# The first input tiles and the first weight chunk in smaller parts, the second linear's chunks split inside the first, rope tables and masks ahead of the third

## The chip, the cores and the metric

The kernel runs on one core of one Trainium2 chip, as one program. The metric is the device time of one execution in microseconds; shown are the median of three runs and one profiled execution. The engines are named as in the profile: PE (TensorE matmul; PEld its weight load), DVE (VectorE), ACT (ScalarE), POOL (GpSimd) and SP (SyncE, which here only issues DMAs).

## The reference

Two layers of a decoder trunk for 256 tokens of width 1024, all in float32. Each layer:

```
h = rmsnorm(x, mix_norm);  z = h @ w_in          # split among three mixers
A: compressed / selected / windowed attention, B: windowed attention with sinks,
C: low-rank attention with a rotary key          # rotary embeddings from positions
g = sigmoid(h @ w_branch_gate)                   # g_a, g_b, g_c
x = x + (g_a*(o_a @ w_a) + g_b*(o_b @ w_b) + g_c*(o_c @ w_c)) @ w_out
x = x + (silu(h2 @ w_gate) * (h2 @ w_up)) @ w_down        # h2 = rmsnorm(x)
x = x + sigmoid(rmsnorm(x) @ w_ple_gate) * (p[i] @ w_ple_proj)
```

and a last rmsnorm. The rotary tables are cos and sin of positions times fixed frequencies.

## The kernel before, in words

**Linears.** Every weight is cut on the host into chunks of 128 partitions by up to 1024 columns, usually two slices k of the contraction by 512 output columns, laid out in the order of use. A float32 product is made of three matmuls on float32r operands: the weight is split into a high part `wh` (a rounded copy by ACT, L276) and a low part `wl` (the difference, by DVE, L281), the activations into `hT` high and low in the same way. For each token tile t (0 or 1, 128 tokens) and each k, `lin` (L331) issues the matmuls high by `wh`, high by `wl`, low by `wh`, in this order (L347 to L349), into a bank `lin` of PSUM. The order over t and k goes in blocks; the first linear alone takes blocks of two k, [2, 2, 2, 2] (L334). The order of the first linears of a layer is `gc0` (a gate), `g1` (low-rank inputs), `g2` (keys, rotated), `g3`, ... (L35). `gc0` has chunks 0 to 3, `g1` 4 to 7, `g2` 8 to 11.

**Chunks.** `load_to` (L253) issues the DMA of a chunk on SP into one of 4 raw buffers; `upper` (L265) issues the `wh` cast and returns a `rest` that issues the `wl` difference and, with it, the load of the chunk four later. There are 6 buffers of high and low parts. A planner (`Plan`, L76) holds modelled times of each engine while the program is written out; `feed` (L285) splits the next chunks as soon as the modelled engines are free, and `W.push` (L138) puts off a piece of work until its modelled inputs are there. `W.until` (L159) lets the model run on until a flag is set. All instructions of an engine run in the order in which they were written out.

**Start.** SP issues in this order: x tile 0 left half, chunk 0, x tile 1 left half, chunk 1, both right halves, chunks 2 and 3 (L387 to L396). ACT issues the constants `con` (identity and frequencies, 176 columns) and the layer parameters `lp`; POOL issues positions, masks (`mload`) and `con2`. PE runs filler matmuls (`warm`, L1268) on a tile of ones, 7, 4 and 4 (L1340). Around them `parts` (L1276) transposes four 128x128 blocks of one input quarter (t, g), multiplies them by the norm's gain on DVE (`xg`, gain from `lp`), casts them on ACT and makes the low part on DVE. `start_1` and `start_2` (L1297, L1305) are hung into the first linear by `script`: they are written out just ahead of the matmuls of (t, k) = (1, 0) and (0, 2) and hold the other input quarters, the splits of chunks 2 to 4, the squares of the rows of x (for the norm's factor `r`, made by POOL in `rsqrt`, L478), the last step of the rotary tables and the masks.

**Rotary tables.** `setup_rope` and `finish_rope` (L421, L446) write a chain of 16 POOL instructions that reduces the angles; `rope_rest` (L454) ends it: a maximum on DVE, one POOL instruction, two sines on ACT (which need another table of functions), and eight copies on POOL to `tabs`. The evacuation of `g2` (`ev_g2`, L662) waits for `tabs`, scales them (`rt`) and rotates; copies `kd` and four or two transposes into a bank `sc` follow.

**Evacuation of the first linear.** `gate` (L639) takes the tanh of the bank on ACT with the scale `rh` = r/2, which POOL makes after `rsqrt`. It is written out right behind the last matmul of its tile, so ACT's later casts stand behind it.

Of the kernel before, what the change touches and what calls it, by code (L numbers as in the profile page):

```python
# [8 lines left out]
F32 = mybir.dt.float32  # L9
F32R = mybir.dt.float32r  # L10
# [7 lines left out]
P = 128  # L18
# [35 lines left out]
RAWB = 4  # L54
# [11 lines left out]
C_ID, C_FREQ, C_FIRST = 0, 128, 176  # L66
# [151 lines left out]
def build(tc, wst, xin, pin, posn, cst, lpar, fnorm, out):  # L218
# [34 lines left out]
    def load_to(n):  # L253
        while st["dma"] < min(n, len(CHUNKS)):
            i = st["dma"]
            off, kk, c = CHUNKS[i]
            r = sb([P, 1024], name="raw", bufs=RAWB, p=wp)
            nc.sync.dma_start(out=r[:, :kk * c],
                              in_=wst[off:off + P * kk * c].rearrange("(p n) -> p n", p=P))
            W.op("D", kk * c * P * 4 / 350e3, [r.tensor.name], [])  # L260
            W.end[r.tensor.name] = ("D", W.t["D"] + 2.0)
            raws[i] = r
            st["dma"] += 1
# [38 lines left out]
    def split_to(n):  # L302
        st["goal"] = max(st["goal"], n)
        feed()
# [26 lines left out]
    def lin(l, name, nk, lhs, evac, blocks=None, wait=0.0, halves=False):  # L331
# [5 lines left out]
        for b in blocks:  # L337
            for t in range(2):
                if t and halves:
                    break  # L340
                for k in range(k0, k0 + b):
# [6 lines left out]
                    T.matmul(out=o, lhsT=xh, rhs=wl, start=False, stop=False)  # L348
                    T.matmul(out=o, lhsT=xl, rhs=wh, start=False, stop=(k == nk - 1))  # L349
# [28 lines left out]
    con = sb([P, C_FIRST], name="con")  # L378
    con2 = sb([P, C_N], name="con2")
# [20 lines left out]
    ident = con[:, C_ID:C_ID + P]  # L400
# [200 lines left out]
    def layer(l, nm, nxt):  # L601
# [120 lines left out]
        step["g2"] = lambda: lin(l, "g2", 8, nm.lhs, ev_g2)  # L722
# [540 lines left out]
    nm = Norm(lps[0][:, L_MIX:L_MIX + 8])  # L1263
# [32 lines left out]

    def start_1():  # L1297
        nm.square(0, 0)
        nm.square(1, 0)
        w2 = split(2)  # L1300
        lo = parts(0, 1)
        w2()
        lo()

    def start_2():  # L1305
        w3 = split(3)
        lo = parts(1, 1)
        w3()
        lo()
        w4 = split(4)  # L1310
        nm.square(0, 1)
        w4()
        nm.square(1, 1)
        rope_t["last"]()
        W.push([], setup_masks, 20.0)
        split_to(HLB)

    warm(WARM[0])
    lo = parts(0, 0)
    w0 = split(0)  # L1320
    lo()
    warm(WARM[1])
    lo = parts(1, 0)
    w0()
    warm(WARM[2])
    w1 = split(1)
    lo()
    w1()
    script[1, 0] = [start_1]
    script[0, 2] = [start_2]  # L1330
    for l in range(DEPTH):
        nm = layer(l, nm, None)
# [7 lines left out]
WARM = (7, 4, 4)  # L1340
# [4 lines left out]
def host_layout(inputs):  # L1345
# [50 lines left out]
    con[:, C_ID:C_ID + P] = np.eye(P)  # L1396
# [37 lines left out]
```

## Time and profile before

| | us |
|---|---|
| median of three runs | 962.79 (962.58 to 962.92) |
| profiled execution, its own time | 962.83 |
| span of the profiled execution | 961.0 |

Times in the rows below count from the start of the span. A row of a timeline has the start, the time taken, the engine, the line of the kernel, the operation, output and inputs by the program's names (buffer numbers left out), shapes and a count. Nearly all instructions show line L214, since a helper records each of them, so they are told apart by tiles. In brackets stands the idle time of the engine before the instruction and what ended it. A matmul's end is modelled and overlaps the next one's start.

### The profile page before, as it was taken

Reading aid. Unit: us, or ns where it says so; the run is one execution under the profiler, and the core shown is the slowest. Engines: PE = TensorE matmul, PEld = TensorE weight load, DVE = VectorE, ACT = ScalarE, POOL = GpSimd, SP = SyncE. Lnnn points to the kernel's source line nnn. Section 1 sums busy time; section 2 is a strip of 40 time slices with the busy share of each in tenths; the row PEclk is TensorE's granted clock in tenths of the full one; section 3 lists DMA queues with packets and bytes.
Section 4 is the critical chain, followed back from the end, with each engine's and each line's share of the span. In section 5 each row is a group of like instructions: output and inputs, shape, how many; then the busy total and the mean of one; then the engine's idle time right before and its main releaser. Section 6 shows DMA issues by size and latency. Waiting matters only on the chain.

```text
span 961.0 us, 13658 instructions
## 1 busy us (share of the span) xinstructions
PE 946.2 (98%) x4867; PEld 781.2 (81%) x4867; DVE 670.1 (70%) x1226; ACT 560.7 (58%) x1015; POOL 53.3 (6%) x104
## 2 busy tenths in 40 slices
PE   8999999999999999999999999999999999999996
PEld 5788888777888888888888898877778888888886
DVE  6696788668776666654767868876886766665554
ACT  6668857666554445443665686766655544444444
POOL 7200000000010000000121000000000000000010
PEclk9999999999999999999999999999999999999999
DMA  8557534525455555657454665254245655555551
GB/s 286 159 162 228 191 102 144 168 88 196 159 187 199 179 176 175 202 170 210 161 173 155 201 200 173 89 175 153 89 154 181 204 190 193 193 179 188 185 175 44
DMA packets 46595, 164.28 MB, mean 171 GB/s; under 512 B 5504, under 2 KB 5760, under 8 KB 46528
## 3 DMA queue, kind: packets, MB, share of 16 engines
q1 hardware_dynamic: 45648, 161.80, 51.5%
q0 software_dynamic: 448, 1.30, 0.4%
q8 instruction: 38, 0.62, 0.3%
q10 hardware_dynamic: 432, 0.32, 0.1%
q14 instruction: 29, 0.24, 0.1%
HBM read 162.35 MB, written 1.05 MB: 170 GB/s over the span
## 4 chain that ended last, share of the span: by engine, by line
PE 95%; POOL 2%; ACT 1%; DVE 1%; issue 1%; ACTq 0%; POOLq 0%
PE lin L214 80%; PE tr L214 7%; PE sc L214 4%; PE pv L214 3%; PE hidps L214 2%; POOL kq L214 1%; POOL ang L214 0%; DVE wl L214 0%; POOL kp L214 0%; DVE um L214 0%; ACT xf L214 0%; DVE khA L214 0%; POOL nsk L214 0%; DVE U L214 0%; ACT pT L214 0%
## 5 line engine op out<-in xcount | busy, mean ns | idle before, releaser
L214 PE MATMUL lin<-wh,hT 128*128 128x512 f32 (+2 forms) x1600 | 512.0, 389 | 0.2 <-ACT wh L214 0.2
L214 DVE TENSOR_TENSOR wl<-raw,wh 128x1024 fp32r<-128x1024 f32 (+2 forms) x308 | 369.1, 1209 | 88.3 <-ACT wh L214 81.8
L214 ACT CAST wh<-raw 128x1024 fp32r<-128x1024 f32 (+2 forms) x308 | 315.7, 1035 | 133.9 <-PE lin L214 124.7
L214 PEld LDWEIGHTS lin<-wh,hT 128*128 128x128 f32 x1600 | 297.1, 188 | 56.7 <-issue 1.5
L214 PE MATMUL lin<-wl,hT 128*128 128x512 f32 (+2 forms) x800 | 305.3, 382 | 2.1 <-DVE wl L214 2.1
L214 PEld LDWEIGHTS lin<-wl,hT 128*128 128x128 f32 x800 | 150.8, 189 | 27.5 <-DVE wl L214 2.7
L214 PE MATMUL lin<-wh,hd 128*128 128x512 f32 x352 | 110.9, 392 | 0.0
L214 PEld LDWEIGHTS lin<-wh,hd 128*128 128x128 f32 x352 | 66.1, 188 | 13.6
L214 PE MATMUL lin<-wl,hd 128*128 128x512 f32 x176 | 68.5, 389 | 0.0
L214 PE MATMUL lin<-wh,oT 128*128 128x512 f32 x192 | 66.3, 400 | 0.0
L214 ACT ACTIVATE th<-lin,rh 128x256 f32<-128x256 f32 (+1 forms) x52 | 26.2, 503 | 65.8 <-PE lin L214 65.8
L214 ACT ACTIVATE p<-p,negm 128x256 f32<-128x256 f32 (+1 forms) x128 | 56.8, 447 | 0.0
L214 DVE SCALAR_TENSOR_TENSOR th<-th,lin 128x256 f32<-128x256 f32 x44 | 18.4, 418 | 49.5 <-ACT th L214 49.5
L214 DVE CUSTOM_DVE_ANT_0 p<-sc,masks 128x128 f32<-128x128 f32 (+1 forms) x96 | 29.5, 353 | 23.0 <-PE sc L214 23.0
L214 ACT COPY pT<-tr 128x512 f32<-128x512 f32 x48 | 28.1, 585 | 27.5 <-PE tr L214 27.1
L214 PEld LDWEIGHTS lin<-wh,oT 128*128 128x128 f32 x192 | 36.1, 188 | 6.9
L214 PE MATMUL lin<-wh,mT 128*128 128x512 f32 x128 | 41.6, 396 | 0.0
L214 POOL TENSOR_SCALAR n0v<-ssq 128x1 f32<-128x1 f32 x7 | 2.1, 304 | 699.9 <-ACT junk L214 699.8
L214 PEld LDWEIGHTS lin<-wl,hd 128*128 128x128 f32 x176 | 33.1, 188 | 6.7
L214 PE MATMUL lin<-wl,oT 128*128 128x512 f32 x96 | 37.5, 391 | 0.0
L214 DVE TENSOR_TENSOR xg<-tr,lp 128x512 f32<-128x512 f32 x28 | 19.3, 690 | 25.2 <-PE tr L214 19.6
L214 ACT CAST hd<-tr 128x256 fp32r<-128x256 f32 x44 | 16.2, 369 | 33.6 <-PE tr L214 33.6
(206 smaller groups left out, 1018.7 us busy)
## 6 DMA issues: line engine op xcount, KB each, us to landing
raw<-wst SPq DMA_DIRECT2D x296, 512.0 KB, 4.2
raw<-wst SPq DMA_DIRECT2D x8, 312.0 KB, 3.1
raw<-wst SPq DMA_DIRECT2D x4, 384.0 KB, 3.1
x<-xin SPq DMA_DIRECT2D x4, 256.0 KB, 6.1
w<-lpar POOLq DMA_DIRECT2D x2, 256.0 KB, 3.7
pr<-pin POOLq DMA_DIRECT2D x2, 256.0 KB, 4.1
fn<-fnorm SPq DMA_DIRECT2D x1, 512.0 KB, 4.1
out<-xf SPq DMA_DIRECT2D x2, 256.0 KB, 2.0
```

The lines of the kernel that those rows point to most:

```text
L214: return fn(*a, **k)
```

## The change

The identity for transposes is no longer loaded with the constants but made on POOL by a memset and a select, ahead of POOL's DMAs; the constants shrink from 176 to 56 columns and now carry the first norm's gain. The load of chunk 0 is cut in two halves, and so are its `wh` and `wl`. The left quarters of x are scaled and split from PSUM in pieces of 128x128: high part on ACT with the gain as scale, low part on DVE. Tile 1's transposes move behind the first three matmuls. In the first linear alone the low activations by `wh` come before the high ones by `wl`. The hooks move to (0, 1), (0, 2), (1, 2), (0, 6) and (1, 6), and the splits of chunks 5, 6 and 7 stand in them. The end of the rotary chain and the masks move to the start of `g2`. Filler matmuls: 7 and 3.

```
@@ -63,7 +63,7 @@
 LEAD, GAP = 128, 256
 
 
-C_ID, C_FREQ, C_FIRST = 0, 128, 176
+C_GAIN, C_FREQ, C_FIRST = 0, 8, 56
 C_CB, C_CM, C_MV, C_S, C_J, C_N = 0, 32, 64, 192, 224, 228
 C_BAND, C_CAUS, C_ALL = 0, 128, 256
 
@@ -255,8 +255,9 @@
             i = st["dma"]
             off, kk, c = CHUNKS[i]
             r = sb([P, 1024], name="raw", bufs=RAWB, p=wp)
-            nc.sync.dma_start(out=r[:, :kk * c],
-                              in_=wst[off:off + P * kk * c].rearrange("(p n) -> p n", p=P))
+            src = wst[off:off + P * kk * c].rearrange("(p n) -> p n", p=P)
+            for o in (slice(0, c), slice(c, kk * c)) if i == 0 else (slice(0, kk * c),):
+                nc.sync.dma_start(out=r[:, o], in_=src[:, o])
             W.op("D", kk * c * P * 4 / 350e3, [r.tensor.name], [])
             W.end[r.tensor.name] = ("D", W.t["D"] + 2.0)
             raws[i] = r
@@ -345,8 +346,9 @@
                     xh, xl = lhs(t, k)
                     o = banks[t][:, :c]
                     T.matmul(out=o, lhsT=xh, rhs=wh, start=(k == 0), stop=False)
-                    T.matmul(out=o, lhsT=xh, rhs=wl, start=False, stop=False)
-                    T.matmul(out=o, lhsT=xl, rhs=wh, start=False, stop=(k == nk - 1))
+                    pair = ((xh, wl), (xl, wh))
+                    for x_, w_ in pair[::-1] if c0 == 0 else pair:
+                        T.matmul(out=o, lhsT=x_, rhs=w_, start=False, stop=(k == nk - 1 and (x_ is xl) == (c0 != 0)))
                     if k == nk - 1:
                         evac(t, banks[t])
                     if t == 1 and (k % kp == kp - 1 or k == nk - 1):
@@ -376,6 +378,10 @@
 
     x = [[sb([P, 512], name=f"x{t}{g}") for g in range(2)] for t in range(2)]
     con = sb([P, C_FIRST], name="con")
+    ident = sb([P, P], name="ident")
+    G.memset(ident, 0.0)
+    G.affine_select(out=ident, in_=ident, compare_op=ALU.not_equal, fill=1.0, base=0, pattern=[[-1, P]],
+                    channel_multiplier=1)
     con2 = sb([P, C_N], name="con2")
     pos = sb([P, 2], I32, name="pos")
     lps = {}
@@ -397,7 +403,6 @@
     mload = sb([P, 2, P], name="mload", tag="kall", bufs=3)
     load(nc.gpsimd, mload, cst[:, C_FIRST + C_N:].rearrange("p (a b) -> p a b", a=2))
     load(nc.gpsimd, con2, cst[:, C_FIRST:C_FIRST + C_N])
-    ident = con[:, C_ID:C_ID + P]
     identr = sb([P, P], F32R, name="identr")
     masks = sb([P, 4, P], name="masks")
     tabs = sb([P, 2, 192], name="tabs")
@@ -719,7 +724,13 @@
                 flags.add(f"U{i}")
             W.push([Uh[i]], rest, 0.0, [uf])
 
-        step["g2"] = lambda: lin(l, "g2", 8, nm.lhs, ev_g2)
+        def step_g2():
+            if l == 0:
+                rope_t["last"]()
+                setup_masks()
+            lin(l, "g2", 8, nm.lhs, ev_g2)
+
+        step["g2"] = step_g2
 
         def ev_g3(t, b):
             rope(b[:, 0:32].rearrange("p (a b) -> p a b", a=1), 1, 16, rt[t][:, 128:192],
@@ -1260,7 +1271,7 @@
         return n4
 
 
-    nm = Norm(lps[0][:, L_MIX:L_MIX + 8])
+    nm = Norm(con[:, C_GAIN:C_GAIN + 8])
     wrm = sb([P, 512], BF16, name="wrm", tag="junk")
     V.memset(wrm, 1.0)
     wps = ps("pv")
@@ -1294,40 +1305,85 @@
             upper(i)
         return late.get(i, lambda: None)
 
+    def tr_x(t):
+        b = ps("tr")
+        for k in range(4):
+            transpose(b[:, k * P:(k + 1) * P], x[t][0][:, k * P:(k + 1) * P])
+        return b, nm.place(t, 0)
+
+    def hi_x(bo, ks):
+        for k in ks:
+            S.activation(out=bo[1][:, 0, k], in_=bo[0][:, k * P:(k + 1) * P], func=AF.Copy, scale=nm.gain[:, k:k + 1])
+
+    def lo_x(bo, ks):
+        for k in ks:
+            V.scalar_tensor_tensor(out=bo[1][:, 1, k], in0=bo[0][:, k * P:(k + 1) * P], scalar=nm.gain[:, k:k + 1],
+                                   in1=bo[1][:, 0, k].bitcast(F32), op0=ALU.mult, op1=ALU.subtract)
+
+
+
+    S.copy(out=small(1, "first", 1), in_=wrm[:, 0:1])
+    warm(WARM[0])
+    x0 = tr_x(0)
+    r0 = raws.pop(0)
+    st["split"] = 1
+    hls[0] = h0, l0 = tuple(sb([P, 1024], F32R, name="w" + p, tag=f"w{p}0") for p in "hl")
+    near, far = (0, 1), (2, 3)
+
+    def half_hi(h):
+        S.copy(out=h0[:, h], in_=r0[:, h])
+
+    def half_lo(h):
+        V.tensor_tensor(out=l0[:, h], in0=r0[:, h], in1=h0[:, h].bitcast(F32), op=ALU.subtract)
+
+    first, second = slice(0, 512), slice(512, 1024)
+    hi_x(x0, near)
+    half_hi(first)
+    lo_x(x0, near)
+    half_lo(first)
+    half_hi(second)
+    half_lo(second)
+    hi_x(x0, far)
+    nm.ok.add((0, 0))
+    warm(WARM[1])
+
     def start_1():
-        nm.square(0, 0)
-        nm.square(1, 0)
+        x1 = tr_x(1)
+        hi_x(x1, near)
+        lo_x(x1, near)
+        lo_x(x0, far)
+        load_to(RAWB + 1)
+        w1 = split(1)
+        w1()
+        hi_x(x1, far)
+        lo_x(x1, far)
+        nm.ok.add((1, 0))
+
+    def start_2():
         w2 = split(2)
         lo = parts(0, 1)
+        lo()
         w2()
-        lo()
-
-    def start_2():
+
+    def start_3():
         w3 = split(3)
         lo = parts(1, 1)
+        lo()
         w3()
-        lo()
+        nm.square(0, 0)
+        nm.square(0, 1)
         w4 = split(4)
-        nm.square(0, 1)
+        nm.square(1, 0)
+        nm.square(1, 1)
         w4()
-        nm.square(1, 1)
-        rope_t["last"]()
-        W.push([], setup_masks, 20.0)
-        split_to(HLB)
-
-    warm(WARM[0])
-    lo = parts(0, 0)
-    w0 = split(0)
-    lo()
-    warm(WARM[1])
-    lo = parts(1, 0)
-    w0()
-    warm(WARM[2])
-    w1 = split(1)
-    lo()
-    w1()
-    script[1, 0] = [start_1]
+        split(5)()
+
+
+    script[0, 1] = [start_1]
     script[0, 2] = [start_2]
+    script[1, 2] = [start_3]
+    script[0, 6] = [lambda: split(6)()]
+    script[1, 6] = [lambda: split(7)()]
     for l in range(DEPTH):
         nm = layer(l, nm, None)
     W.until(lambda: len(sent) == 2)
@@ -1337,7 +1393,7 @@
 SPACE = 4.2
 SLACK = 0.9
 TWO = "ga"
-WARM = (7, 4, 4)
+WARM = (7, 3)
 NEAR = 2
 WAIT = 1.5
 
@@ -1393,7 +1449,7 @@
     lp = np.ascontiguousarray(np.stack(lp))
     i = np.arange(P)
     con, con2, con3 = (np.zeros((P, n), np.float32) for n in (C_FIRST, C_N, C_ALL))
-    con[:, C_ID:C_ID + P] = np.eye(P)
+    con[:, C_GAIN:C_GAIN + 8] = lp[0][:, L_MIX:L_MIX + 8]
     con3[:, C_CAUS:C_CAUS + P] = np.where(i[None, :] <= i[:, None], 0, NEG)
     con3[:, C_BAND:C_BAND + P] = np.where(i[None, :] > i[:, None], 0, NEG)
     fr = [10000.0 ** (-np.arange(0, d, 2) / d) for d in (64, 32)]
```

## Rows read from the trace of the kernel before

**Rows 1.** The page, part 1: busy time, share of the span and instructions of each engine.

```profile
PE 946.2 (98%) x4867; PEld 781.2 (81%) x4867; DVE 670.1 (70%) x1226; ACT 560.7 (58%) x1015; POOL 53.3 (6%) x104
```

**Rows 2.** The busy time of each engine in the stretch from 10 to 20 us, its instructions, the granted clock, the DMA share and GB/s.

```profile
10.00:20.00 10.00, 9.82 (x47) 8.13 (x48) 9.08 (x12) 8.49 (x16) 9.14 (x13) 1.00 0.81 295
```

**Rows 3.** What TensorE waited for between 0 and 30 us: total us, times, longest us.

```profile
PE lin L214 <- DVE wl L214: 2.1, 2, 1.2
...
PE lin L214 <- ACT wh L214: 0.2, 1, 0.2
```

**Rows 4.** The same view from 30 us to the end, its longest entry.

```profile
PE sc L214 <- ACT kTC L214: 1.1, 2, 0.6
```

**Rows 5.** The timeline of the SP queue from 0 to 45 us (start us, us, queue, line, operation): its first input half, first weight chunk, second weight chunk.

```profile
0.72 0.38 SPq L373 DMA_DIRECT2D x<-xin  x1
1.16 0.42 SPq L258 DMA_DIRECT2D raw<-wst  x1
...
2.10 0.44 SPq L258 DMA_DIRECT2D raw<-wst  x1
```

**Rows 6.** DMA issues of three narrow stretches (0.5 to 1, 1 to 1.3 and 1.8 to 2.3 us), with KB and us from issue to landing: the first input half, the first weight chunk, the second weight chunk.

```profile
x<-xin SPq DMA_DIRECT2D x1, 256.0 KB, 3.6
...
raw<-wst SPq DMA_DIRECT2D x1, 512.0 KB, 4.7
...
raw<-wst SPq DMA_DIRECT2D x1, 512.0 KB, 7.0
```

**Rows 7.** The timeline of all engines, the start: start us, us, engine, line, operation, count, and in brackets the idle time before it and what ended it.

```profile
4.60 0.66 PE L214 MATMUL tr<-con,x 128*128 128x128 f32 x4 [0.17 <-DMA con<-cst]
...
6.13 0.69 DVE L214 TENSOR_TENSOR xg<-tr,lp 128x512 f32<-128x512 f32 x1 [4.75 <-DMA lp<-lpar]
...
8.48 0.50 PE L214 MATMUL lin<-wh,hT 128*128 128x512 f32 x1
...
10.18 0.50 PE L214 MATMUL lin<-wl,hT 128*128 128x512 f32 x1 [1.20 <-DVE wl L214]
```

**Rows 8.** Instruction groups by shape, of ScalarE: count, busy us, mean ns of one.

```profile
L214 ACT CAST wh<-raw 128x1024 fp32r<-128x1024 f32 x296 | 307.1, 1047 | 132.4 <-PE lin L214 124.0 <-DMA raw<-wst 4.3 <-DVE mg L214 2.2
...
L214 ACT CAST hT<-xg 128x512 fp32r<-128x512 f32 x24 | 14.8, 619 | 26.1 <-DVE xg L214 26.1
...
L214 ACT ACTIVATE v<-lin,n0y 128x128 f32<-128x128 f32 x2 | 0.7, 370 | 0.0
```

**Rows 9.** The same view, of VectorE.

```profile
L214 DVE TENSOR_TENSOR wl<-raw,wh 128x1024 fp32r<-128x1024 f32 x296 | 359.4, 1224 | 80.9 <-ACT wh L214 74.4 <-issue 0.3
...
L214 DVE TENSOR_TENSOR cs_s<-sc,cs_s 128x128 f32<-128x128 f32 x4 | 1.2, 291 | 0.1
```

**Rows 10.** The timeline of all engines, around the end of the first linear and in the second.

```profile
18.09 0.39 PE L214 MATMUL lin<-wl,hT 128*128 128x512 f32 x1
...
18.77 0.39 PE L214 MATMUL lin<-wl,hT 128*128 128x512 f32 x1
...
20.70 1.28 ACT L214 ACT_TABLE_LOAD   x1
...
22.42 0.28 ACT L214 ACTIVATE cs<-kq 128x96 f32<-128x96 f32 x1 [0.44 <-POOL kq L214]
...
24.69 0.69 ACT L214 ACTIVATE gateC<-lin,rh 128x512 f32<-128x512 f32 x1
...
25.23 1.38 POOL L214 COPY tabs<-cs 128x64 f32<-128x64 f32 x8
25.27 1.04 ACT L214 CAST wh<-raw 128x1024 fp32r<-128x1024 f32 x1
...
26.37 0.49 PE L214 MATMUL lin<-wh,hT 128*128 128x512 f32 x1 [0.19 <-ACT wh L214]
...
27.74 0.50 PE L214 MATMUL lin<-wl,hT 128*128 128x512 f32 x1 [0.88 <-DVE wl L214]
...
28.78 0.62 PE L214 MATMUL lin<-wh,hT 128*128 128x512 f32 x2
```

**Rows 11.** The timeline of GpSimd from 0 to 26 us.

```profile
6.43 0.18 POOL L214 CAST pf<-pos 128x2 f32<-128x2 int32 x1 [3.22 <-DMA pos<-posn]
...
12.34 0.45 POOL L214 TENSOR_SCALAR kp<-kq 128x96 f32<-128x96 f32 x1
...
13.33 1.32 POOL L214 TENSOR_SCALAR kp<-kq 128x96 f32<-128x96 f32 x1
...
21.06 1.33 POOL L214 TENSOR_SCALAR kq<-kq 128x96 f32<-128x96 f32 x1
22.48 0.32 POOL L214 TENSOR_SCALAR n0v<-ssq 128x1 f32<-128x1 f32 x1
...
23.54 0.24 POOL L214 TENSOR_SCALAR rh<-n0y 128x1 f32<-128x1 f32 x1
...
25.08 0.21 POOL L214 MEMSET masks<- 128x128 f32 x1
```

**Rows 12.** The timeline in the third linear: the rotation of its first evacuated tile, the copies after it, and the transposes of those copies on TensorE.

```profile
41.04 0.69 DVE L214 TENSOR_TENSOR ra<-lin,rt 128x512 f32<-128x512 f32 x1 [0.81 <-PE lin L214]
...
43.16 0.93 ACT L214 COPY kd<-kall 128x512 f32<-128x512 f32 x2 [4.26 <-DVE kall L214]
...
44.92 0.82 PE L214 MATMUL sc<-con,kd 128*128 128x128 f32 x6
```

## Prediction

> **What bounds the kernel now.** I read the busy shares first: TensorE (PE) is busy 946.2 us of the 961.0 us span [rows 1]. I then asked what PE waited for. After 30 us its longest single wait is 0.6 us and the largest group sums to 1.1 us [rows 4], so nothing behind 30 us is worth a change, and work saved on the other engines there is free cover. Before 30 us it loses 2.1 us to VectorE's low parts of weights (`wl`) and 0.2 us to ScalarE's high parts (`wh`) [rows 3], and before that it does no useful matmul until 8.48 us [rows 7]. So the change can move the end by what PE gains or loses in the first 30 us, one for one, and by what it disturbs later. The granted clock is 1.00 from 10 to 20 us, the full level of 2.4 GHz, after the seven filler matmuls at the start [rows 2]; I count no term for it.
>
> The same stretch shows VectorE busy 9.08 of 10 us, ScalarE 8.49 and GpSimd 9.14 [rows 2]: the start is nearly bound by all of them at once. A new order of work there mostly trades one wait for another, and that is where I expect most of an earlier start to go.
>
> **The pitch.** Two successive `wl` matmuls stand 0.68 us apart with two others between [rows 10], so one matmul of 512 columns is 0.227 us of PE. A linear of 48 is 10.9 us.
>
> **Where I measure.** The last place where the old prologue loses time is the fourth weight chunk of the second linear. The `wh` cast for it starts at 25.27 behind the tanh of the gate at 24.69, which stands behind two table loads (1.28 us each) and the sines. PE waits at 26.37 and again at 27.74 [rows 10]. The first matmul of token tile 1 of the second linear is the second of the pair at 28.78, so it starts 0.23 later, at 29.01. I work out when the changed kernel reaches that matmul.
>
> **The start, step by step.** The first input half lands at 0.72 + 3.6 = 4.32 us [rows 5, 6]. Before, the four transposes started at 4.60 because the constants with the identity came last [rows 7]; the identity is now made on GpSimd while the input is on its way. The memset of 128x128 is 0.21 us [rows 11]; the select has no row. Its lower bound is 0.2, its upper bound the slowest GpSimd row of 96 columns, 1.33 us [rows 11], taken to 128 columns: 1.8 us. I take 0.3, near the memset, since VectorE is idle then; either way it is ready before 4.32. So the transposes run at 4.47, bound by the filler matmuls, and end 0.66 later, at 5.13. The gain vector now comes with the small constants, so the wait of VectorE for `lp` until 6.13 [rows 7] goes. ScalarE then makes two pieces of 128x128 (0.37 us each, the form of `v<-lin` [rows 8], the second starting about 0.1 before the first ends): 5.17 to 5.81. The half-chunk cast of 512 columns costs what `hT` costs, 0.62 [rows 8]: 5.71 to 6.33. The half chunk is there by then, since the whole chunk landed at 1.16 + 4.7 = 5.86 [rows 5, 6]. First real matmul: 6.37 instead of 8.48, **2.1 us earlier**. The `wl` matmul, now third, waits for VectorE: 6.37 + 0.69 (a line between 0.29 at 128 and 1.22 at 1024 columns [rows 9]) = 7.06; stall 0.3 instead of the 1.2 idle before 10.18 [rows 7]. The split of the load in two costs one more issue slot on SP, 0.42 to 0.44 us [rows 5], for everything behind it; the second chunk is late by its transfer anyway (next step), so I take 0 and keep 0.4 as the bound.
>
> **The rest of the first linear.** I walked the three queues in program order with these durations. The second chunk landed at 2.10 + 7.0 = 9.1 us [rows 5, 6], which an earlier start does not speed up; `wh` 9.1 to 10.1, `wl` 10.1 to 11.4, while PE arrives at 10.8: stall 0.6. Behind it VectorE has the order low part of the input, `wl`, gain product, low part, `wl`, and twice waits about 0.8 for a ScalarE cast in between: stalls 0.6 before the third `wl`, 0.4 and 0.5 for the last input tile. Sum of stalls 2.4. Three groups of four transposes that stand in the stream cost 0.47 each, 1.4 in all. The first linear ends at 6.37 + 10.9 + 1.4 + 2.4 = 21.05. Before: counting 18 matmuls back from the first lost slot of the second linear (26.37 less 0.35 idle, so 26.02) gives 21.93. Of the 2.1 us won at the start **0.9 is left here**.
>
> **The second linear.** Its chunks 4 to 7 are now split inside the first; the sines, two table loads (1.28 each [rows 10]) and masks stand behind it and no longer precede the gate's tanh. What is late next is the tanh's scale, `rh`, from GpSimd, since the cast of chunk 7 stands behind that tanh. Before, `rh` ended at 23.78, 1.30 after its chain began at 22.48 [rows 11]. The last range-reduction step in front of it (1.33 at 21.06) moves away; the position load waits for the identity, +0.5. So `rh` = 23.78 - 1.33 + 0.5 = 22.95; tanh 22.99 to 23.68; cast to 24.63; `wl` to 25.91; PE arrives at 25.4: stall 0.6. The twelve matmuls of chunks 4 and 5, and all others of tile 0, add 24 x 0.227 = 5.45: 21.05 + 5.45 + 0.58 = 27.08, against 29.01: **1.93 us earlier**.
>
> That `rh` takes GpSimd's pace as before. The same GpSimd instruction took 0.45 us at 12.34 and 1.32 us at 13.33 [rows 11], and the slow ones fall on VectorE's `wl`. From `pf` at 6.43 to the moved step at 21.06 [rows 11] 18 instructions take 14.6 us; at 0.45 each they would take 8.1, so 6.5 is stretch. VectorE was busy 0.91 of that time [rows 2]; in my walk it waits about 5 of 15 us, so 0.67: a quarter of the stretch, 1.6 us, goes. Then `rh` is no longer last, the stall of 0.6 goes, and the end is 26.5: **2.5 us**. The Trainium skill (GPSIMD Engine Reference, 1. Specifications) says that GpSimd shares its SBUF interfaces with VectorE and contends with instructions of two SBUF inputs; by that the sum is 2.5, by an unchanged pace 1.93, and the trace agrees (0.45 against 1.32). I take 2.2 between them.
>
> **The third linear.** The chain of position tables now starts with it: a maximum on VectorE, a step on GpSimd (up to 1.33 [rows 11]), a table load 1.28, two sines of 0.28 and eight copies of 1.38 in all [rows 10], with 0.3 for the maximum: 4.8 us. It starts at 32.5 (29.01 - 2.2 + 24 matmuls and a group of transposes) and ends at 37.3 if nothing stands in front on ScalarE; the rotation that needs it starts at 41.04 - 2.2 = 38.8 [rows 12]. It is hidden, with 1.5 us to spare, and the second table load falls into ScalarE's idle time ahead of the next tanh. I cost it at 0. The masks are needed far later: 0. The dummy copy on ScalarE only occupies an idle engine: 0. Swapping the order of the second and third matmul in the first linear is what makes the late `wl` cheap, and is in the stalls above.
>
> **Sum.** The profiled execution took 962.83 us (961.0 of span and 1.83 around it); the median of the runs is 962.79, so they agree. 962.83 - 2.2 = **960.6 us**. A measurement of this kernel can tell about 0.2% from no change, 1.93 us here, so my own two ends (1.93 and 2.5) lie on and just over that line.
>
> **Rivals.**
>
> A, *the start runs nearly without stalls.* PE could reach the matmul at 6.37 + 72 x 0.227 + 1.4 = 24.1 if all 2.4 us of stalls went. For it: mask and constant loads now enter later, the small constants are 60 KB less, so the second chunk can land earlier. Against it: VectorE's order. With half the stalls gone the gain is 3.6: 959.2. Chance 0.17.
>
> B, *the table chain is late and PE waits in the third linear.* ScalarE may have in front of the sines an evacuation, two squares and two casts, 3.2 us; then the tables are 1.7 late. The copies of the rotated tile end at 44.09 and PE's transposes of them start at 44.92 [rows 12], which leaves 0.8: PE waits 0.9. Gain 1.3: 961.5. Chance 0.2. The Trainium skill (ScalarE: Activation LUTs, Rules for kernel authors) budgets about 2.7 us for each switch of tables. By that the wait would be 1.4 longer and the gain gone, about 962.8. The trace disagrees: the tanh starts at 24.69 right after a load that took 1.28.
>
> C, *GpSimd's `rh` comes a microsecond later than 22.95,* through a late position load. Then chunk 7 waits as before and the gain is 0.9: 961.9. Chance 0.08.
>
> D, *slower: the identity comes late.* Everything now starts from a select on GpSimd. From 4.47 us on, each microsecond that it is late delays every matmul by one. Break-even is 6.7 us, and from 8.6 us on the kernel is slower by over 0.2%. It would have to take 7 us from GpSimd's start at 1.2, four times the bound from the slowest row. Time: about 965. Chance 0.05.
>
> **How the numbers follow.** My own case has 0.5; with ends at 1.6 and 2.8, three quarters of it lie beyond the line: 0.38. With A: faster 0.55. Same: 0.12 + B 0.2 + C 0.08 = 0.40. Slower: D, 0.05. The range leaves out D and the far half of A: from 959.0 to 962.5, which takes in B by the trace, C, and the extra SP slot. The likeliest case alone is 960.0 to 961.2.
>
> **What would show it.** First matmul of the first linear near 6.4; three or four PE waits of 0.3 to 0.6 for `wl` or the last input tile between 10 and 18; no table load before the gate's tanh; that tanh near 22 to 23; tile 1 of the second linear from 26.5 to 27.1; no PE wait of over 0.5 from 30 to 50. I am wrong if the stalls between 7 and 21 sum to under 1 or over 3.5, or if PE waits for the key copies in the third linear.

## The result: slower by 6.5 us, and the profile after

The changed kernel takes 969.21 us (median of four runs, 967.41 to 970.18) against 962.71 before: ratio 1.0065, 95% interval 1.0048 to 1.0083. Its profiled execution took 969.15, with a span of 967.4 against 961.0. I had forecast 960.6.

**The start came as forecast.** The first real matmul runs at 6.16 [rows 7 have 8.48], GpSimd's `rh` ends at 20.59 [rows 11 have 23.78], and the second linear's tile 1 starts at 26.56, 2.44 us earlier than before. TensorE, ScalarE and GpSimd in the timeline of all engines of the changed kernel (the identity first):

```profile
0.72 0.20 POOL L214 MEMSET ident<- 128x128 f32 x1 [0.29 <-POOLq L1482]
1.00 0.29 POOL L214 TENSOR_SCALAR_AFFINE_SELECT ident<-ident 128x128 f32<-128x128 f32 x1
...
6.16 0.73 PE L214 MATMUL lin<-wh,hT 128*128 128x512 f32 x2 [0.57 <-ACT wh L214]
...
20.36 0.23 POOL L214 TENSOR_SCALAR rh<-n0y 128x1 f32<-128x1 f32 x1
...
21.75 0.67 ACT L214 ACTIVATE gateC<-lin,rh 128x512 f32<-128x512 f32 x1
...
27.50 1.04 ACT L214 CAST wh<-raw 128x1024 fp32r<-128x1024 f32 x1 [2.37 <-DMA raw<-wst]
28.45 0.68 ACT L214 ACTIVATE zc<-lin,n0y 128x512 f32<-128x512 f32 x1
...
29.18 0.66 PE L214 MATMUL tr<-ident,zc 128*128 128x128 f32 x4 [1.11 <-ACT zc L214]
```

The last three rows are the first loss: ScalarE waits 2.37 us for the transfer of chunk 9, whose cast stands in front of the evacuation `zc`, and TensorE waits for `zc`. The load of a chunk is issued behind the `wl` of the chunk four earlier; here that `wl` ends at 22.16, so the load of chunk 9 is issued at 22.18 and lands 5.2 us later. Before, it was issued at 21.02 and took 4.8.

What TensorE waited for up to 30 us, where [rows 3] had 2.1 for `wl`:

```profile
PE tr L214 <- ACT zc L214: 1.1, 1, 1.1
PE lin L214 <- ACT wh L214: 0.6, 1, 0.6
PE lin L214 <- DVE wl L214: 0.4, 1, 0.4
```

**Then more than everything is lost between 46 and 66 us.** What TensorE waited for from 30 us to the end; [rows 4] had 1.1 as its longest sum and 0.6 as its longest wait:

```profile
PE tr L214 <- ACT dup L214: 2.4, 2, 2.2
PE lin L214 <- DVE wl L214: 2.0, 2, 1.6
PE sc L214 <- ACT kTC L214: 1.1, 2, 0.6
PE tr L214 <- ACT pT L214: 0.9, 2, 0.4
PE sc L214 <- DVE khA L214: 0.8, 1, 0.8
```

The stretches from 40 to 70 us (busy us of PE, PEld, DVE, ACT, POOL; granted clock; DMA share; GB/s). From 10 to 20 us, where [rows 2] had VectorE at 9.08 and ScalarE at 8.49, they now stand at 7.98 and 7.22.

```profile
40.00:50.00 10.00, 8.81 (x49) 7.39 (x48) 7.37 (x18) 4.06 (x10) 2.18 (x5) 1.00 0.25 67
50.00:60.00 10.00, 8.07 (x51) 7.10 (x49) 7.30 (x20) 5.92 (x11) 0.62 (x3) 1.00 0.55 187
60.00:70.00 10.00, 8.09 (x30) 6.63 (x31) 7.49 (x14) 5.00 (x10) 0.20 (x1) 0.83 0.49 162
```

The timeline of all engines from the third linear into the fourth (`g3`, chunks 12 to 15, the matmuls of 312 columns, from 45.73). The low parts `wl` of chunks 14 and 15 (47.36, 52.17) come behind the rotation of the third linear's tile 1 (45.36) and the key work; TensorE waits for them and for what stands behind them:

```profile
38.81 2.05 POOL L214 COPY tabs<-cs 128x64 f32<-128x64 f32 x8 [1.51 <-ACT cs L214]
...
40.97 0.68 DVE L214 TENSOR_TENSOR ra<-lin,rt 128x512 f32<-128x512 f32 x1
...
45.36 0.69 DVE L214 TENSOR_TENSOR ra<-lin,rt 128x512 f32<-128x512 f32 x1 [1.71 <-PE lin L214]
...
47.36 0.80 DVE L214 TENSOR_TENSOR wl<-raw,wh 128x624 fp32r<-128x624 f32 x1
48.22 0.41 PE L214 MATMUL lin<-wl,hT 128*128 128x312 f32 x1 [0.38 <-DVE wl L214]
...
49.58 0.63 PE L214 MATMUL sc<-ident,kd 128*128 128x128 f32 x4 [0.81 <-DVE khA L214]
...
52.17 1.94 DVE L214 TENSOR_TENSOR wl<-raw,wh 128x624 fp32r<-128x624 f32 x2
...
53.03 0.41 PE L214 MATMUL lin<-wl,hT 128*128 128x312 f32 x1 [1.60 <-DVE wl L214]
```

Before, both `wl` (one merged row) stood ahead of that rotation; VectorE's timeline of the kernel before:

```profile
44.73 1.53 DVE L214 TENSOR_TENSOR wl<-raw,wh 128x624 fp32r<-128x624 f32 x2 [1.61 <-ACT wh L214]
...
47.16 0.69 DVE L214 TENSOR_TENSOR ra<-lin,rt 128x512 f32<-128x512 f32 x1 [0.41 <-PE lin L214]
```

And the evacuation of the fourth linear: the second table load, the copies `dup` behind it, the transposes that wait for them, and matmuls at half their pace:

```profile
57.24 1.28 ACT L214 ACT_TABLE_LOAD   x1 [3.50 <-DVE rb L214]
58.53 0.28 ACT L214 ACTIVATE gat<-lin,rh 128x24 f32<-128x24 f32 x1
...
58.85 0.18 DVE L214 TENSOR_SCALAR gat<-gat 128x24 f32<-128x24 f32 x1 [1.39 <-ACT gat L214]
...
59.32 2.00 ACT L214 CAST wh<-raw 128x1024 fp32r<-128x1024 f32 x2
61.20 0.30 ACT L214 ACTIVATE gat<-lin,rh 128x24 f32<-128x24 f32 x1
61.37 0.49 ACT L214 ACTIVATE dup<-lin,n1y 128x256 f32<-128x256 f32 x1
...
61.91 0.62 PE L214 MATMUL tr<-ident,dup 128*128 128x128 f32 x3 [2.24 <-ACT dup L214]
...
63.19 1.05 PE L214 MATMUL lin<-wh,hT 128*128 128x512 f32 x2
```

To see where each microsecond goes I set the n-th matmul of the linears (`lin<-wh` and `lin<-wl`, 3552 in each trace) beside the n-th of before. Start in the trace of the kernel named less start before, in us, one profiled run each:

| matmul, start before | after | e1 | e2 | e3 | e5 | e6 | e7 | e9 | f7 | f5 |
|---|---|---|---|---|---|---|---|---|---|---|
| 0, 8.48 | -2.32 | -1.75 | 0.04 | -1.78 | -2.08 | -1.60 | -1.79 | -2.04 | -1.43 | -1.61 |
| 67, 27.74 | -2.31 | 1.22 | -1.47 | -2.21 | -1.63 | -2.04 | -1.74 | -2.01 | -1.80 | -1.95 |
| 80, 31.28 | -1.14 | 2.36 | -1.31 | -1.68 | -1.06 | -1.32 | -0.89 | 0.08 | -0.20 | -2.10 |
| 144, 46.96 | -1.23 | 2.81 | -1.44 | -1.77 | -1.16 | -1.28 | 0.44 | 1.57 | -0.19 | -2.08 |
| 168, 51.41 | 2.44 | 5.04 | 2.24 | 1.91 | 2.51 | -1.28 | 0.46 | 5.25 | -0.16 | -1.33 |
| 201, 57.80 | 4.42 | 4.14 | 4.23 | 2.62 | 3.22 | 0.53 | 0.98 | 7.24 | 0.36 | -0.63 |
| 215, 61.09 | 6.00 | 7.56 | 5.83 | 2.64 | 3.23 | 0.56 | 1.00 | 7.25 | 0.38 | -0.63 |
| 900, 275.53 | 5.89 | 8.86 | 5.76 | 2.48 | 3.16 | 0.48 | 0.90 | 7.21 | 0.31 | -0.68 |
| 3300, 893.94 | 6.18 | 9.20 | 5.80 | 1.51 | 3.55 | 0.74 | -0.08 | 7.50 | -0.58 | -1.55 |
| end of the span | 6.35 | 9.38 | 5.81 | 1.68 | 3.72 | 0.92 | 0.08 | 7.68 | -0.40 | -1.38 |

Each linear has 48 matmuls, so 96 to 143 are the third linear's and 144 to 167 the first tile of the fourth. Read down the column "after": 2.3 won, 1.2 lost at `zc`, 3.7 in the fourth linear's first tile (the three waits shown sum to 2.8; the rest lies at the matmuls around them, which overlap less: 0.25 from the one at 48.22 to the next, where 0.14 is usual), 2.0 at `dup`, 1.6 behind it at the lower clock. That last piece is eight matmuls: a pair took 1.05 instead of 0.62 (63.19 above), and the granted clock of that stretch is 0.83, full level for most of it and 1.2 GHz for the rest.

The rows 900 and 3300 show a difference that stands far behind the last edited instruction. Between them every kernel that has an added one-column tanh (e3, e7, e10, f1, f2, f4, f5, f7, all below) gains 0.87 to 0.99 us on the kernel before; e2 stays level (0.03), and all others lose 0.26 to 0.39. Between e6 and f7 no single matmul behind 215 brings more than 0.05: it is a small difference of pace over hundreds of matmuls. What in the added call brings it no run shows. Where a kernel of the first group is compared with one of the last, about 1.2 us is this and has nothing to do with the order or the table load.

### The profile page after: what moved, and what is told of

Its sections match the earlier page's. It is cut to its first block, busy times and chain, and to the rows that moved or that the text cites. A ratio compares the mean times of both kernels' runs of the same rounds, so it can differ in the third digit from the quotient of the medians.

```text
span 967.4 us, 13660 instructions
## 1 busy us (share of the span) xinstructions
PE 948.4 (98%) x4862; PEld 781.6 (81%) x4862; DVE 669.5 (69%) x1231; ACT 562.2 (58%) x1023; POOL 53.1 (5%) x106
## 3 DMA queue, kind: packets, MB, share of 16 engines
HBM read 162.29 MB, written 1.05 MB: 169 GB/s over the span
## 4 chain that ended last, share of the span: by engine, by line
PE 94%; ACT 2%; DVE 2%; DMA 2%; issue 1%; SPq 0%; ACTq 0%; DVEq 0%
PE lin L214 79%; PE tr L214 7%; PE sc L214 4%; PE pv L214 3%; PE hidps L214 2%; DMA raw<-wst 1%; DVE wl L214 1%; ACT wh L214 0%; DMA con<-cst 0%; DVE um L214 0%; ACT junk L214 0%; DVE khA L214 0%; ACT xf L214 0%; ACT dup L214 0%; DVE U L214 0%
## 5 line engine op out<-in xcount | busy, mean ns | idle before, releaser
L214 DVE TENSOR_TENSOR wl<-raw,wh 128x1024 fp32r<-128x1024 f32 (+3 forms) x309 | 368.8, 1205 | 88.8 <-ACT wh L214 82.5
L214 ACT CAST wh<-raw 128x1024 fp32r<-128x1024 f32 (+3 forms) x309 | 316.1, 1034 | 136.0 <-PE lin L214 125.0
L214 DVE TENSOR_TENSOR p<-p,sm 128x512 f32<-128x512 f32 x48 | 33.2, 692 | 1.7
```

Source lines behind the costliest of these rows:

```text
L214: return fn(*a, **k)
```

## The experiments

Each kernel was timed against the kernel before (962.7 to 962.9 in all of them). In the expectations the waits for `wl` and `khA` at 48 to 53 us are put in the third linear; they are in the fourth. "Chunk 11's cast" in f4's is chunk 13's.

**Which part of the change? e1 puts the tables and masks back, e2 moves only them.** e1 is the changed kernel with

```
-        def step_g2():
-            if l == 0:
-                rope_t["last"]()
-                setup_masks()
-            lin(l, "g2", 8, nm.lhs, ev_g2)
-
-        step["g2"] = step_g2
+        step["g2"] = lambda: lin(l, "g2", 8, nm.lhs, ev_g2)
...
         split(5)()
+        rope_t["last"]()
+        W.push([], setup_masks, 20.0)
```

and e2 is the kernel before with the opposite edit and nothing else.

> The changed kernel with the end of the table chain and the masks back inside the first linear, where they were before; all else as changed. Theory 1 (the loss comes from moving the table chain into the third linear: what it puts late there and in the fourth linear is 7.4 us between 47 and 66 us): 961 to 963 us, with no wait of PE over 1 us between 45 and 66 us. Theory 2 (the new start is to blame: later chunks are loaded and split later): 967 to 969 us, the waits stay.

> The kernel before with that one move alone: table chain and masks at the third linear. Theory 1: the losses of the third and fourth linear without the gain of the start, 966 to 971 us. Theory 2: 962 to 963.5 us, since the start is as before.

Measured: e1 971.83 (ratio 1.0090, 1.0074 to 1.0107), e2 966.94 (1.0046, 1.0031 to 1.0061). e2 has the start of before and, to within 0.01 us, the four waits of the changed kernel:

```profile
48.01 0.41 PE L214 MATMUL lin<-wl,hT 128*128 128x312 f32 x1 [0.38 <-DVE wl L214]
...
49.37 0.63 PE L214 MATMUL sc<-con,kd 128*128 128x128 f32 x4 [0.81 <-DVE khA L214]
...
52.83 0.41 PE L214 MATMUL lin<-wl,hT 128*128 128x312 f32 x1 [1.60 <-DVE wl L214]
...
61.72 0.55 PE L214 MATMUL tr<-con,dup 128*128 128x128 f32 x3 [2.25 <-ACT dup L214]
```

So the move of the tables alone makes the loss between 46 and 66. (e2's profiled run, 968.61, is its slowest; the other three lie between 966.8 and 967.0 and have no trace.) But e1 refutes the simple half of my theory, that the rest would then be won. With the new start the rope's end may not go back to this place, behind the split of chunk 5, either:

```profile
23.12 1.33 POOL L214 TENSOR_SCALAR kq<-kq 128x96 f32<-128x96 f32 x1 [4.15 <-DVE kq L214]
...
25.76 0.24 POOL L214 TENSOR_SCALAR rh<-n0y 128x1 f32<-128x1 f32 x1
```

GpSimd waits 4.15 us for VectorE's maximum, which stands behind the chunks now split there, and `rh` stands behind that: it ends at 26.0 instead of 20.6, the gate waits, and TensorE waits 1.67 for `wh` at 27.70. At matmul 67 e1 is 1.22 behind the kernel before, where the changed kernel is 2.31 ahead. This is my rival C, 3 us later than its 22.95 instead of one. It is not all of e1's loss: behind matmul 144 another 6 us go, with the tables early (more on this at e10).

**What about the move? e3 takes the reload off the chain, e5 every table load.** e3 is the changed kernel with a one-column tanh behind the sines; e5 has copies in their place.

```
             S.activation(out=cs[:, 1], in_=ang, func=AF.Sin)
+            S.activation(out=small(1, "back", 1), in_=half[:, 0:1], func=AF.Tanh)
```

> The changed kernel with one tanh of one column right behind the sines, so that the second table load falls there (ScalarE idle from 39.5 to 43 us) and not ahead of the gate's tanh at 57 us. If that load is on the chain of the 2.24 us wait at 61.9 and of the clock that falls after it: 1.3 us less wait and 1 to 1.6 us less at the lower clock, 966 to 967 us. If the wait is only the order of the instructions: 969 us.

> The changed kernel with the two sines replaced by copies (the rotary tables hold other numbers), so no table load at all but the first; the order of all instructions as changed. If the time of the two loads is what hurts: 965 to 966.5 us. If it is the order in which the late table chain makes the planner write the splits: the waits for wl at 48.2 and 53.0 us stay, 966.5 to 968 us.

Measured: e3 964.82 (1.0021, 1.0012 to 1.0030), e5 966.70 (1.0040, 1.0025 to 1.0055). In both the wait for `dup` is 0.97 instead of 2.24 and the granted clock from 60 to 70 is 1.00, and in both the waits for `wl` (2.0 in two) and `khA` (0.8) are untouched. TensorE's timeline of e3:

```profile
60.11 0.55 PE L214 MATMUL tr<-ident,dup 128*128 128x128 f32 x3 [0.97 <-ACT dup L214]
```

In e5 no table is loaded behind the start, so the untouched waits are not the load's. By the table, the load and the clock behind it are 2.8 of e3's 4.7 (matmuls 168 to 215: 0.73 lost instead of 3.56), which is what its first figure expected. That e3 lies below both figures comes from elsewhere: 0.5 at `zc` and 1.3 of the pace behind matmul 900. e5 lies in the range of the order theory: each half of the loss is real, and neither is the whole.

**The order that the planner writes: e6 and e7.** `ev_g2` makes the model of time wait for `tabs`, and the scaling `rt` books the modelled VectorE until behind that. `feed` holds back the low part of a chunk more than two ahead while VectorE is booked more than 0.9 ahead, so `wl` of chunks 14 and 15 was written behind the rotation of tile 1; before, it stood ahead. e6 is the changed kernel with the lateness hidden from the model, e7 is e3 with the same line.

```
+            W.end[tabs.tensor.name] = ("G", 0.0)
             V.tensor_scalar(out=rt[t], in0=tabs[:, t, :], scalar1=nm.r[t], scalar2=None, op0=ALU.mult)
```

> The changed kernel, with one line that hides from the planner that the rotary tables come late; the order written out in the third linear is then the old one (the last two weight chunks' low parts ahead of the rotation of tile 1), and the second table load is still in front of the tanh of the fourth linear. Order theory: the waits for wl at 48 and 53 and for khA at 49.6 go, which is 3.5 to 4.0 of the loss, and the time is 965.2 to 965.7 if the load keeps its 4.4; if the earlier order also takes the load off the chain, down to 961.5. Load theory (the load and the clock behind it are all that matters): 968 to 969.

> The changed kernel with the same line and a one-column tanh right behind the sines, so that ScalarE has its old table back long before the fourth linear. If order and reload are the whole loss, the gain of 1.2 us that stood at the end of the third linear holds to the end: 961.5 (961.0 to 962.3), no wait of PE over 0.6 from 30 to 70, granted clock 1.00 throughout. If something else of the change costs time there, it stays above 963.

Measured: e6 963.89 (1.0015, 1.0006 to 1.0025), e7 962.65 (0.9998, 0.9990 to 1.0007). In e6 the gain of 1.28 passes the third linear and the fourth's first tile untouched (table, matmuls 80 to 168): the order was worth 5.3 us of 969.2. That is the 3.7 of the waits and the 1.6 of the clock, which stays at 1.00 although the load is still on the chain: the wait at `dup` is shorter. The 1.6 of the clock goes with either mend, so e3's gain and e6's do not add up.

```profile
58.03 0.55 PE L214 MATMUL tr<-ident,dup 128*128 128x128 f32 x3 [1.81 <-ACT dup L214]
```

e7 missed its 961.5. There both loads stand in front of the cast of chunk 13 (40.58 instead of 38.65 in e6), VectorE's `wl` for it stands in front of `rt`, and the first rotation is late:

```profile
45.30 0.88 PE L214 MATMUL sc<-ident,kd 128*128 128x128 f32 x6 [1.11 <-ACT kd L214]
```

Up to matmul 215 e7 is behind e6 (1.00 against 0.56); that its median is 1.2 lower comes from the pace behind matmul 900.

**The clock: e9** puts 18 fillers of 256 columns in front of the second transposes of `dup`.

```
...
+            if l == 0 and i == 1:
+                wp2 = ps("pv")
+                for _ in range(18):
+                    nc.tensor.matmul(out=wp2[:, 0:256], lhsT=fil[:, 0:P], rhs=fil, start=True, stop=True)
             b = ps("tr")
```

> The changed kernel with 18 filler matmuls of 256 columns (2.0 us by the 0.227 us of 512) in PE's order right ahead of the second transposes of dup, where PE waits 2.24 us. If the fall of the clock costs time of its own beyond the wait, the granted clock stays at 1.00 from 60 to 70 and the time is 967.4 to 967.9 (1.6 less, the ledger's rise from 62.2 to 65.7). If the clock falls anyway or costs nothing, 969 or later.

Measured: 969.09, but the four runs are two pairs, 967.2 and 967.7, 970.5 and 970.6. The profiled one is of the upper pair. In it the clock from 60 to 70 is 1.00 and no time is lost behind `dup` (table: 7.24, 7.25), as expected; but it had lost 1.6 us in another place, behind a longer wait for `zc`:

```profile
30.00:40.00 10.00, 9.60 (x39) 7.85 (x40) 6.50 (x10) 7.44 (x18) 3.56 (x8) 0.83 0.50 152
...
60.00:70.00 10.00, 9.73 (x55) 7.86 (x55) 6.47 (x17) 7.38 (x12) 0.83 (x3) 1.00 0.54 172
```

So the fall costs 1.6 us of its own, and in this trace the fillers kept it away at `dup`. By its median e9 stands at the rival's figure, 969, all the same. That the lower pair had no such wait at `zc` fits, but those runs have no trace.

**Another place for the tables: e10** has the end of the rope and the masks at the start of the second linear, and e3's tanh.

```
...
+        def step_g1():
+            if l == 0:
+                rope_t["last"]()
+                setup_masks()
+            lin(l, "g1", 8, nm.lhs, ev_g1)
```

> The changed kernel with the end of the rotary tables and the masks at the start of the second linear instead of the third, and the one-column tanh behind the sines. The tables are then early for the planner too and no line hides anything. Order and reload theory: the waits of the third and fourth linears go; the two loads and the sines (3.2 us on ScalarE from about 26) stand in front of the evacuation of the second linear's tile 0 and the casts of the third linear, so some of the gain is lost there: 961.5 to 963.5. If the place of the tables did not matter: 964 or more.

Measured: 970.63 (1.0080, 1.0067 to 1.0094), at the rival's open end, but because the place matters. I had counted most of the loads' 3.2 us as hidden. `zc` stands right behind them, at 31.52, and TensorE waits 3.11 for it:

```profile
32.24 1.11 PE L214 MATMUL tr<-ident,zc 128*128 128x128 f32 x4 [3.11 <-ACT zc L214]
```

Against the kernel before, that turns 2.5 won (matmul 80) into 1.5 lost (81). Another 4.8 are lost between matmuls 143 and 287, although the tables are ready early: the cast of chunk 15 stands behind tile 1's key copies (52.92 behind 52.09), TensorE waits 1.17 for it at 53.68, and four waits for `wl` of 0.3 to 1.1 follow. e1 has the same copies, cast and wait at the same times. So early tables alone don't bring the old order back; what else puts that cast there wasn't tried.

**All causes away: f4, f7, then f1, f2, f5.** In e6 ScalarE is idle 1.71 us ahead of tile 1's key copies. f4 is e6 with the one-column tanh there, reading a column of the rotation's own PSUM bank; f7 is the same with `half[:, 0:1]`, a small tile of SBUF, in place of `b[:, 0:1]`.

```
             kall[t] = sb([P, 8, 64], name="kall", bufs=3)
+            if l == 0 and t == 1:
+                S.activation(out=small(1, "back", 1), in_=b[:, 0:1], func=AF.Tanh)
```

> e6 (the old order in the third linear) with the one-column tanh at the rotation of tile 1, in ScalarE's idle time ahead of the copies kd of that tile, instead of behind the sines. The reload then stands neither in front of chunk 11's cast (as in e7) nor on the chain of dup (as in e6). Load theory: the wait for dup falls from 1.8 to about 0.5 and the time from 963.9 to 962.6, by the 1.28 of the load. Rival (the wait for dup comes from VectorE's release of the bank, not from the load): 963.9 again.

> f4 with the one-column tanh reading a small tile of SBUF instead of a column of the rotation's bank. In f4 and f1 VectorE's rotation of tile 1 started only behind that tanh (48.35), and PE then waited 1.5 to 2.2 for POOL's dup; if that is because both read one bank of PSUM, the wait goes here. Load theory: the order is e6's and the 1.28 of the load is off the chain of dup, so the wait for dup at 58 falls from 1.8 to 0.5 and the time to 962.4 to 962.6. Rival (that wait is VectorE's release): 963.5 as f4.

Measured: f4 963.48 (1.0010, 1.0000 to 1.0019), f7 961.37 (0.9984, 0.9975 to 0.9993). f4's tanh held up the rotation itself; ScalarE and VectorE in f4, then ScalarE in f7:

```profile
48.28 0.17 ACT L214 ACTIVATE back<-lin 128x1 f32<-128x1 f32 x1
48.48 0.69 DVE L214 TENSOR_TENSOR ra<-lin,rt 128x512 f32<-128x512 f32 x1 [1.83 <-ACT back L214]
...
50.60 0.92 ACT L214 COPY kd<-kall 128x512 f32<-128x512 f32 x2 [2.15 <-DVE kall L214]
```

```profile
47.94 1.28 ACT L214 ACT_TABLE_LOAD   x1
49.23 0.20 ACT L214 ACTIVATE back<-half 128x1 f32<-128x1 f32 x1
49.63 0.93 ACT L214 COPY kd<-kall 128x512 f32<-128x512 f32 x2 [0.19 <-DVE kall L214]
```

The program lets two engines at one PSUM bank only one after the other, two readers too. The Trainium skill (PSUM — Partial Sum Buffer, PSUM bank collisions raise a hardware error) says that such accesses collide even as reads, so the order is needed; no run here shows a collision, only what the order costs. That also explains the row at 57.24: the tanh `gat` may read its bank only after VectorE's `rb`, and the load in front of it waited the 3.50 us with it, instead of using them. Between matmuls 168 and 201, e6 loses 1.81 and f7 0.52: the difference, 1.29, is the load's 1.28. By the medians f7 is 2.5 below e6, where 1.3 to 1.5 was expected. The other 1.2 is the pace behind matmul 900, which the load doesn't touch: there f7's trace wins 0.89 and e6's loses 0.26. In the two profiled runs it is hidden, since f7's is the slowest of its eleven (962.40; the fastest is 960.01), with a wait for `zc` of 1.53.

f1 and f5 also keep chunk 9's cast behind `zc`, and split chunks 14 and 15 ahead of tile 1's rotation; f1 has f4's tanh, f5 f7's. f2 is f1 with the masks 6 us later.

```
-            if i >= min(st["goal"], len(CHUNKS)) or ...
+            if i >= min(st["goal"], st.get("cap", 9), len(CHUNKS)) or ...
...
             S.activation(out=zc, in_=b, func=AF.Copy, scale=nm.r[t])
+            st["cap"] = len(CHUNKS)
...
             if l == 0 and t == 1:
+                for i in (14, 15):
+                    chunk(i)
```

> f4, and the cast of chunk 9 may not be written ahead of the evacuation zc of the second linear's tile 0 (chunks 14 and 15 are split ahead of tile 1's rotation, as before). If zc stood late only because that cast waits for its DMA, PE's wait at 29.2 (0.6 to 2.0) goes and the gain is still 2.0 at the start of the third linear. Then either it holds to the end: 960.7; or the table chain is late next, as my rival B had it, by 0.8 to 1.0: 961.6. If the transfers set the pace instead (chunks 10 and 11 late as well), 962.6 as f4.

> f1 with the two copies of the masks (0.9 us on ScalarE ahead of the table load) put off by 6 us. If the table chain is the next thing late, the tables come 0.9 earlier and the wait for kd shrinks by that: 960.7 to 961.0. If it is not, the same time as f1.

> f1 with the same mend: old order in the third linear, reload in ScalarE's idle time, zc ahead of chunk 9's cast. In f1 the gain at 43 us was 2.3, all that the start had won, with no wait for kd. If the three costs are the whole loss, 2.2 less than f1's 963.4: 961.2, with only the second wait for dup (up to 0.9) left; if the table chain (rival B) takes part back, 961.5 to 962.2. If it is 962.5 or more, a fourth cost is there.

Measured: f1 963.39 (1.0007, 0.9999 to 1.0016), f2 963.89 (1.0010, 1.0001 to 1.0019), f5 961.42 (0.9987, 0.9979 to 0.9996). f1 and f2 have f4's fault, so their times tell little; f2's masks were not what held the table load. In f5 the wait for `zc` is gone and the start's gain, 2.1, reaches the end of the third linear. What TensorE waits for in f5 from 26 to 100 us:

```profile
PE tr L214 <- ACT dup L214: 0.9, 1, 0.9
PE sc L214 <- ACT kTC L214: 0.6, 1, 0.6
PE tr L214 <- POOL dup L214: 0.5, 1, 0.5
```

f7 and f5 are faster than the kernel before by 0.16 and 0.13%, which is 1.4 us each. About 0.9 of that is again the pace behind matmul 900: at matmul 215 f7's trace is 0.38 behind the kernel before, f5's 0.63 ahead. So f5 keeps 0.6 of the 2.1 us that its start had won, and no kernel here keeps all of it. Against f7 the mend of `zc` won nothing by the median; it narrowed eleven runs from 2.4 to 1.1 us. Where f5's last 1.4 us goes is seen (the two waits for `dup`), not tried.

## Why the prediction was wrong

**The start: right.** First matmul forecast at 6.37, found at 6.16. The select took 0.29, I took 0.3.

**The rest of the first linear: right.** Its end was forecast at 21.05; the first matmul of the next linear runs at 21.12. The stalls, by the same subtraction (21.12 - 6.16 - 10.9 - 1.4), are 2.7, I had 2.4. The waits that stand at matmuls sum to only 0.7 of that (0.38 at 15.05 for `wl`, 0.28 at 17.09 for the last input tile); others stand at the weight loads in front of them (0.46 at 8.93 and 0.48 at 16.31, both for input tiles).

**The second linear: right up to tile 1.** I took 2.2 between 1.93 and 2.5, found 2.44. The reason for the upper end held in part: `rh` came at 20.6, not 22.95, with VectorE at 7.98 of 10 us (my walk had 6.7). Of these 2.4 us, 1.0 is the position load, which let `pf` start at 5.91, 0.5 earlier than before, where I had it 0.5 later: that was luck. From `pf` to the end of `nsk` GpSimd then took 12.35 instead of 14.73 us, 2.4 less where I had 1.6, and 0.9 of that was lost again in `rsqrt` (`n0y` 1.51 instead of 0.57). What I left out stands in the same linear: that its evacuation `zc` has the cast of chunk 9 in front. I had asked only what the earlier TensorE waits for until 29 us. The start came earlier, but the load of chunk 9 was issued 1.2 us later than before, behind a later `wl` of chunk 5, and landed at 27.4 instead of 25.8, so ScalarE now sat 2.37 us in front of a chunk not yet there. Chunk 9 isn't needed until after the transposes of `zc` (its first matmul, 102, runs at 35.53).

**"The third linear ... I cost it at 0": the step that failed.** The table chain moved ahead of the third linear cost 7.2 us in the trace instead of 0, between matmuls 144 (1.23 ahead) and 215 (6.00 behind): waits for `wl`, `khA` and `dup`, and the lower clock. e2, which moves it alone, loses 7.3 there. Three things in the step were wrong.
- *The chain's end.* I put it from 32.5 to 37.3 for a need at 38.8. It began at 34.78 (the maximum stood behind two `wl`), ScalarE had the squares, the masks and a cast in front of the load (37.17), the copies took 2.05: it ended at 40.86. I had written "if nothing stands in front on ScalarE". Rival B had priced that lateness at a wait of 0.9 for the key copies; the trace of the changed kernel does not show that wait. The chain was late, as B had it, but what the lateness cost stood at other places and was several times its size.
- *The order.* The kernel's order is computed from modelled times, so a step that is late in the model moves work elsewhere. I followed the instructions that the change moves, and took the rest of the order as it was. e6 shows this as the largest term, 5.3 us with the clock.
- *"The second table load falls into ScalarE's idle time ahead of the next tanh."* ScalarE was idle, 3.50 us, but the load waited too. VectorE's scaling of `gat` then waited 1.39, and all behind it. On the chain it costs 1.3. The Trainium skill (ScalarE: Activation LUTs, Rules for kernel authors) budgets 2.7 for a switch. The trace disagrees (load 1.28, tanh 0.01 behind it, at 58.53). Where the switch stands counts for more than its price: in e7, right behind the sines, it held up the cast of chunk 13.

**The clock** was in no part of the prediction: I counted no term because [rows 2] showed 1.00. One of the waits that I missed, 2.24 us at `dup`, was followed by a fall to 1.2 GHz that cost 1.6 us.

**The signs I had named.** The first matmul, the tanh with no load in front (21.75, I had 22 to 23) and tile 1 came as listed. Of the three or four waits from 10 to 18 there were two, of 0.38 and 0.28. "No PE wait of over 0.5 from 30 to 50" did not hold (0.81 at 49.58), and that line pointed at the right stretch. Neither of the two things by which I said that I would be wrong happened: the stalls came to 2.7 and no wait for the key copies is in the trace. They watched the start and one wait, and the loss came by another way.

**The chances.** I gave slower 0.05, on one mechanism, the identity, which took 0.29 us. The rival that I needed was that a table chain moved next to its use changes who waits for whom in that stage.

## What to carry to other kernels

Where the order of instructions is computed from a model, diff the emitted order of each engine over the whole kernel, not only the moved lines; here a late value in the model cost more than the late value on the chip. When two kernels differ far behind the edit, take that off before reading the difference of their medians. Put a switch of function tables where its next function has no wait of its own, for instance by a one-column call on a tile of SBUF in real idle time. When the start gets faster, look at what is fed by transfers that do not: the evacuation that TensorE needs next shouldn't stand behind a cast of data not yet landed.

## What the runs showed of the hardware

- A table load waits with the function call it precedes: 3.50 us idle, then 1.28 of load (57.24). With a call that has no wait it started at once (47.94 in f7).
- The granted clock fell at waits of TensorE of 2.24 (after, 0.83 in 60 to 70), 2.25 (e2, the same stretch), 2.02 (e9, 0.83 in 30 to 40), 3.11 (e10, the same stretch) and 2.76 us (f2, 0.66 in 50 to 60), and in e1 behind 1.67 and 0.76 with one matmul between them (0.85 in 30 to 40). It did not at 1.81 (e6) and, in f1, not at 2.22. In after, e2 and e9 the fall cost 1.6 us in eight or nine matmuls at 1.2 GHz. Why f1 kept its clock stays open.
- Eleven runs of f7 lie 2.4 us apart, and the four of the changed kernel 2.8. In the traces the wait for `zc` differs from 0.5 (e3) to 2.0 (e9) with the landing of chunk 9. That this is the whole scatter isn't shown.
- With no wait to explain it, the same matmuls ran at slightly different paces in different kernels: between matmuls 900 and 3300 f7 was 0.89 us ahead of the kernel before and e6 0.26 behind it. The kernels fall into groups by whether they have the added one-column call; the cause stays open.
